# A list scheduler that counts eight transfers under way on SyncE's queue: one return trip in eight transfers instead of three, and pieces in another order

## The chip, the cores and the metric

The kernel runs on one core of one Trainium2 chip. The metric is the time of one execution on the device in microseconds (us). The kernel before took 271.07, 270.63 and 270.41 us in three runs, median 270.63. Another execution, not one of these three, was profiled: 271.06 us.

## The reference

The reference is a trunk of two layers over 256 tokens with D = 1024 features, all in fp32. Each layer normalises x, projects it to ten column groups with one matrix, runs three groups of attention heads side by side, gates them and projects back:

```python
for layer in range(DEPTH):
    h = rms_norm(x, norm_g[layer])
    proj = jnp.einsum('btd,dc->btc', h, w_in[layer])
    sb_q, sb_k, sb_v, sb_g, mb_q, mb_k, mb_v, mb_g, mem_q, mem_g = jnp.split(proj, split_at, axis=-1)
    o_sb = stick_breaking_attention(sb_q, sb_k, sb_v) * jax.nn.silu(sb_g)
    o_mb = moba_attention(rotary(mb_q), rotary(mb_k), mb_v) * jax.nn.silu(mb_g)
    m = rms_norm(mem, mem_norm_g[layer])
    mk, mv = jnp.split(jnp.einsum('bmd,dc->bmc', m, w_mem_kv[layer]), 2, axis=-1)
    o_mem = memory_attention(mem_q, mk, mv) * jax.nn.silu(mem_g)
    mixed = jnp.concatenate([o_sb, o_mb, o_mem], axis=-1)
    x = x + jnp.einsum('btc,cd->btd', mixed, w_out[layer])
return rms_norm(x, final_norm_g)
```

(The splitting into heads is left out.) There are six sb heads (stick breaking), six mb heads (here one causal softmax, since 256 tokens are one block) and four mem heads, which look at 256 memory tokens; a head has 64 features.

## The kernel before

**Products.** A product in fp32 is made of three matmuls in a narrower type. Every operand is split into a high part (a cast) and a low part (the operand less the cast), and hi x hi, hi x lo and lo x hi are summed in one PSUM bank. Where a piece is named in `DBL`, the high and low parts of the weights lie side by side, and one matmul of 512 columns and one of 256 do the work of three of 256.

**Weights.** They come from HBM in 114 chunks of 768 columns or so (128 partitions). A chunk is loaded into one of six raw buffers (`dma_chunk`, its DMA is issued at L366 on SyncE's queue), cast to its high part on ScalarE or VectorE (`hi_task`, L275), and the low part is subtracted on VectorE (`lo_task`, L281). Seven pairs of high and low parts are held (`hl`). The load of the next chunk into a raw buffer is issued when the subtraction that read that buffer is done, so a load on SyncE's queue often waits for VectorE.

**Attention.** Heads are worked on in pairs: sb 0 to 2, mb 0 to 2, mem 0 and 1. `pair_scores` makes the scores of a pair on TensorE in a smaller matmul shape (64 rows). Softmax or stick breaking then run on ScalarE and VectorE. The weights of the attention must be transposed for the second product. This is done in two steps. `pair_turn` transposes blocks of 32 x 32 on VectorE into a tile D (L843). Then `trip` writes D to a tile Z in memory outside the core's own (the *dump*, L996) and reads it back with the blocks in place (the *return*, L1007), into F or T; the profile prints F and T for the same kind of tile, by the name under which its memory was set up. The return is four transfers, one for each 32 partitions, or eight of half the size where the trip's name stands in `HALVES`. `pair_task` makes the second product (weights x values) in the shape 128 x 64, and then on VectorE multiplies it with the gate and splits it into mxhi and mxlo for the output projection (wo0, wo1, wo2).

**What sets the order.** The kernel is built by a list scheduler (`Sched`). Each task is a generator that says which engine, which buffers and which named values its next step needs. The scheduler holds a clock per engine and a cost model, and again and again picks the step that can start first; among steps that can start within a slack (`SLACK`, `SLACK_PE`) the lower priority number wins (`PRI`, `P_*`). The weights' chunks follow the list `ORDER` of each layer; `SCG` and `PVG` say which pairs' scores and second products are made together, `GATES` which gate columns are worked on together; `HOLD` and `SPARE2` bound how long and with how many banks a group is held back. The hardware then runs each engine's list in that order, and semaphores keep it correct. In the cost model a transfer occupies SyncE for 450 ns and then a shared bandwidth (`queue`), whatever number of transfers is under way.

**Around the change.** SyncE's queue holds 170 rows: weight loads, x and memory loads (`uT<-xT`, `uT<-memT`), dumps and returns. Near 80 to 120 us of the profile, the trips of the three mb pairs and the two mem pairs of layer 0 stand there between the loads of layer 1's memory tokens (memT, four transfers) and those of w_out.

Of the kernel before, what the change touches and what calls it, by code (L numbers as in the profile page):

```python
# [27 lines left out]
RAW = 6  # L28
KORD = ((4, 5, 0, 1, 2, 3, 6, 7), (6, 7, 4, 5, 0, 1, 2, 3))
LAT_SAME, LAT_CROSS = 130.0, 240.0  # L30
PE_LATE = 368.2
NORM_LATE = 542.1
DG_LATE = 1595.9
COLD = 3900.0
PRI = {"sb": (12, 16), "mb": (2, 14), "mem": (54, 40)}
P_EV = 37
P_H0 = -8
P_RX = 27
P_M0 = 62
P_RM = 2  # L40
P_M1 = 55
URG = 2
X_AT = {5: 4, 6: 5, 7: 6, 8: 7}
CST_AT = 12
X0_AT = 6
X1_AT = 13
DMA_GBS = 330.0
SP_ISSUE = 450.0
POOL_ISSUE = 1000.0
POOL_TRIP = 5500.0  # L50
DMA_LAT = 2200.0
DMA_GBS_1K = 285.0
TRIP_LAT = 1500.0
MEM_AT = 1
ORDER = (["sb_qk", "mb_k", "mb_q", "mem_q", "mv", "sb_g", "mk", "mb_v", "mb_g", "sb_v", "mem_g"],
         ["mv", "mk", "mb_q", "mb_k", "mem_q", "sb_q", "sb_k", "mb_g", "mb_v", "sb_v", "mem_g", "sb_g"])
GATES = {"sb_g": ((0,), (1,), (2,)), "mb_g": ((0, 1), (2,)), "mem_g": ((0,), (1,))}
SCG = (((("mem", 1), ("mb", 0), ("sb", 2)), (("sb", 0), ("sb", 1)), (("mb", 1),), (("mb", 2), ("mem", 0))),
       ((("sb", 1), ("mb", 2), ("sb", 2)), (("sb", 0), ("mb", 0), ("mb", 1)), (("mem", 0), ("mem", 1))))
PVG = (((("mem", 0), ("mem", 1)), (("mb", 0), ("mb", 2), ("mb", 1), ("sb", 2)), (("sb", 1), ("sb", 0))),  # L60
       ((("sb", 2),), (("mb", 2), ("sb", 0), ("sb", 1)), (("mb", 0), ("mb", 1), ("mem", 1), ("mem", 0))))
HOLD = 25950.0
HALVES = [("F", 0, "mem", 0), ("F", 0, "mb", 1), ("F", 0, "mb", 2)]
CROWD = 1
SPARE1 = 2
SPARE2 = 1
SUMP = (1, 2)
DBL = (("mem_g", 0), ("mb_g", 1), ("mb_g", 0), ("mem_q", 1), ("mk", 1), ("sb_qk", 0), ("sb_q", 1), ("mk", 0), ("sb_g", 1))
DVE_W = 231.1
AHEAD = 1  # L70
DVE_HI = 718.2
SLACK_PE = 7.9
SLACK = 64.5


def _free(ap):
    n = 1
    for d in ap.shape[1:]:
        n *= d
    return n  # L80
# [18 lines left out]
class Sched:  # L99
# [37 lines left out]
    def _avail(self, k, eng):  # L137
# [21 lines left out]
        if cond is not None and not cond():  # L159
            return None  # L160
        return t + r.get("late", PE_LATE) if eng == "pe" and k.gen.__name__ != "main" else t

# [59 lines left out]
def hybrid_trunk(ctx: ExitStack, tc: tile.TileContext, x, mem, norm_g, w_in, w_mem_kv, w_out,  # L222
# [5 lines left out]
    S = Sched()  # L228
# [131 lines left out]
    def queue(nbytes, run, now):  # L360

        dma_t["t"] = max(dma_t["t"], now) + nbytes / (380.0 if run >= 3072 else DMA_GBS if run > 1024 else DMA_GBS_1K)
        return dma_t["t"] + DMA_LAT

    def dma(dst, src, name=None, q=None, now=0.0):
        (q or nc.sync).dma_start(dst, src)  # L366
        if q is None:
            S.T["sp"] = max(S.T["sp"], now) + SP_ISSUE
        t = queue(_free(dst) * 4 * dst.shape[0], dst.shape[-1] * 4, now)
        if name:  # L370
            S.ready[name] = t

# [239 lines left out]
    def norm_task(l, t, H, done):  # L612
# [3 lines left out]
        for q in range(2):  # L616
            s = slice(q * 512, (q + 1) * 512)
            _, (w,) = yield R("dve", need=[("gb", 0)], alloc=["w"])
            stt(w, src[:, s], r, gb[:, s], OP.mult, OP.mult)
            _, (pt,) = yield R("pe", alloc=["bank"], late=NORM_LATE)  # L620
            for i in range(4):
# [370 lines left out]
    def trip(D, F, e, name, need=(), alloc=()):  # L992

        _, (Z,) = yield R("sp", alloc=["Z"])
        Zv = Z[:, :4 * e]
        nc.sync.dma_start(Zv, D[:, :4 * e])  # L996
        S.op("sp", SP_ISSUE)
        t = queue(2048 * e, 4096, S.cur.t) + TRIP_LAT
        S.res["D"].items.append((t, None, D))
        S.ready[("dump",) + name] = t  # L1000
        _, bufs = yield R("sp", need=[("dump",) + name] + list(need), alloc=alloc)
        F = bufs[0] if alloc else F
        Fv = F[:, :4 * e].rearrange("p (i e) -> p i e", i=4)
        for j in range(4):
            for i0 in range(0, 4, 2 if name in HALVES else 4):
                i1 = i0 + (2 if name in HALVES else 4)
                nc.sync.dma_start(Fv[32 * j:32 * j + 32, i0:i1],  # L1007
                                  Zv.rearrange("(i r) (j e) -> j r i e", i=4, j=4)[j, :, i0:i1])
                S.op("sp", SP_ISSUE)
        t = queue(2048 * e, 1024, S.cur.t) + TRIP_LAT  # L1010
        S.res["Z"].items.append((t, None, Z))
        S.ready[name] = t
        return F
# [90 lines left out]
    def main():  # L1104
# [26 lines left out]
        for l in range(DEPTH):  # L1131
# [34 lines left out]
            for h in range(SBH):  # L1166
                S.spawn(sb_head(l, h) if sums(l, "sb", h // 2) else scan_head(l, h), PRI["sb"][1] + h)
            for h in range(MEMH):
                S.spawn(soft_head(l, h, "mem"), PRI["mem"][1] + h)
            for h in range(SBH):  # L1170
                S.spawn(soft_head(l, h, "mb"), PRI["mb"][1] + h)
            for kind, n in (("sb", 3), ("mb", 3), ("mem", 2)):
                for c in range(n):
                    S.spawn(pair_scores(l, kind, c), PRI[kind][0] + 2)
                    S.spawn(pair_sums(l, c) if sums(l, kind, c) else pair_turn(l, kind, c), PRI[kind][0] + 1)
                    S.spawn(pair_task(l, kind, c), PRI[kind][0])
            if l == 0:
# [145 lines left out]
```

## Time and profile before

| | |
|---|---|
| time of the profiled execution | 271.06 us |
| its span, first to last instruction | 269.0 us |
| median of three other runs | 270.63 us (270.41 to 271.07) |
| TensorE matmuls (PE) | 261.0 us, 97% |
| TensorE weight loads (PEld) | 241.0 us, 90% |
| VectorE (DVE) | 229.4 us, 85% |
| ScalarE (ACT) | 197.9 us, 74% |
| GpSimd (POOL) | 7.3 us, 3% |
| granted TensorE clock | 0.995 of full speed |
| moved by DMA | 65.49 MB, mean 243 GB/s |

The difference of 271.06 and 269.0 lies around the span. In the rows of the profile a line starts with the start time and the length in us; `x8` is the number of instructions; `out<-in` are the tiles that an instruction writes and reads; a bracket at the end is the time its engine sat idle ahead of it and what ended that. SPq is SyncE's queue, which issues DMAs; a row of it tells how long the issue took, not the transfer.

### The profile page before, as it was taken

The page shows a single profiled execution, that of the slowest core. Times are in us where ns is not written, and L with a number is a line of the kernel's source. Part 1 is how long each engine was busy: PE and PEld are TensorE (multiplying, and loading weights), DVE is VectorE, ACT ScalarE, POOL GpSimd, SP SyncE. Part 2 cuts the span into 40 slices and gives each one's busy share as a digit, 9 for nine tenths or more (in the row PEclk, how much of TensorE's full clock was granted, in tenths as well). Part 3 has the DMA queues.
Part 4 walks back from the last instruction along what each step waited for, and adds up shares of the span by engine and source line. Part 5 has one row for each costly group of instructions (what it writes and reads, how often), then busy time and mean ns, then how long its engine had stood idle before and what let it go on. Part 6 is the DMA issues. An engine that isn't in the chain of part 4 may idle for free.

```text
span 269.0 us, 5193 instructions
## 1 busy us (share of the span) xinstructions
PE 261.0 (97%) x1733; PEld 241.0 (90%) x1733; DVE 229.4 (85%) x532; ACT 197.9 (74%) x462; POOL 7.3 (3%) x19
## 2 busy tenths in 40 slices
PE   8999999999999997999999999999999999999992
PEld 5889999999898995998999999889989989889991
DVE  4778889999999997995889678699999999996282
ACT  3798786799989897681887446476999995985053
POOL 0002100100000000000000000000000000000000
PEclk9999999999999999999999999999999999999998
DMA  7999989988858779894588755867899896964004
GB/s 219 363 403 395 387 279 286 322 255 287 239 190 251 244 197 333 267 251 159 133 272 283 234 182 219 274 207 247 268 265 267 271 305 178 279 232 139 0 0 156
DMA packets 50665, 65.49 MB, mean 243 GB/s; under 512 B 4240, under 2 KB 46608, under 8 KB 50640
## 3 DMA queue, kind: packets, MB, share of 16 engines
q1 hardware_dynamic: 49552, 63.08, 73.9%
q0 software_dynamic: 512, 1.31, 1.6%
q10 hardware_dynamic: 576, 0.79, 0.9%
q8 instruction: 13, 0.21, 0.3%
q14 instruction: 12, 0.10, 0.1%
HBM read 56.51 MB, written 8.65 MB: 242 GB/s over the span
## 4 chain that ended last, share of the span: by engine, by line
PE 94%; DMA 2%; ACT 1%; DVE 1%; SPq 1%; issue 0%; DVEq 0%
PE bank L258 93%; DMA T<-Z 2%; PE bank L264 1%; SPq L1007 1%; ACT ga L277 0%; ACT ss L277 0%; ACT junk L277 0%; DVE ga L285 0%; DVE xs L289 0%; DVE gT L281 0%; DVE st L809 0%; DVEq L1319 0%; SPq L366 0%; DVE junk L1107 0%; ACT sb_v L277 0%
## 5 line engine op out<-in xcount | busy, mean ns | idle before, releaser
L281 DVE TENSOR_TENSOR hl<-raw,hl 128x768 fp32r<-128x768 f32 (+3 forms) x114 | 101.4, 897 | 9.3 <-ACT hl L275 8.8
L258 PE MATMUL bank<-T,hl 128*128 128x256 f32 (+1 forms) x662 | 106.7, 320 | 0.0
L258 PEld LDWEIGHTS bank<-T,hl 128*128 128x128 f32 x662 | 94.1, 192 | 10.2 <-issue 1.8
L275 ACT CAST hl<-raw 128x768 fp32r<-128x768 f32 (+2 forms) x108 | 83.9, 795 | 11.2 <-PE bank L258 8.2
L258 PE MATMUL bank<-hl,T 128*128 128x384 f32 (+1 forms) x480 | 80.7, 325 | 0.0
L258 PEld LDWEIGHTS bank<-hl,T 128*128 128x128 f32 x480 | 78.5, 188 | 1.0 <-issue 0.4
L258 PE MATMUL bank<-hl,mxhi 128*128 128x384 f32 (+1 forms) x192 | 45.0, 318 | 0.0
L258 PEld LDWEIGHTS bank<-hl,mxhi 128*128 128x128 f32 x192 | 33.3, 189 | 0.6 <-issue 0.6
L258 PE MATMUL bank<-hl,mxlo 128*128 128x384 f32 (+1 forms) x96 | 30.4, 317 | 0.0
L277 ACT ACTIVATE w<-w,st 128x256 f32<-128x256 f32 (+1 forms) x44 | 18.9, 464 | 2.4 <-DVE st L796 2.2
L277 ACT ACTIVATE junk<-xs 128x384 bf16<-128x384 f32 (+2 forms) x15 | 8.0, 531 | 16.6 <-DVE xs L281 16.0
L277 ACT ACTIVATE ga<-ga 128x256 f32<-128x256 f32 (+1 forms) x42 | 18.5, 446 | 1.1 <-DVE ga L285 0.7
L258 PEld LDWEIGHTS bank<-hl,mxlo 128*128 128x128 f32 x96 | 18.1, 189 | 0.1
L843 DVE STREAM_TRANSPOSE D<-w 128x384 f32<-128x384 f32 (+1 forms) x28 | 17.0, 606 | 0.9 <-ACT w L277 0.9
L277 ACT ACTIVATE T<-uT,gc 128x256 fp32r<-128x256 f32 x24 | 11.5, 500 | 2.1 <-DMA uT<-xT_dram 2.1
L285 DVE SCALAR_TENSOR_TENSOR T<-uT,gc,T 128x256 fp32r<-128x256 f32 x24 | 11.5, 478 | 0.7 <-ACT T L277 0.7
L281 DVE TENSOR_TENSOR xs<-bank,xs 128x384 f32<-128x384 f32 (+1 forms) x11 | 5.7, 518 | 7.2 <-PE bank L258 7.1
L277 ACT ACTIVATE a<-a 128x384 f32<-128x384 f32 x24 | 11.8, 523 | 0.1
L281 DVE TENSOR_TENSOR ev<-bank,gT 128x256 f32<-128x256 f32 x16 | 6.6, 417 | 4.2 <-PE bank L258 4.1
L277 ACT ACTIVATE a<-bank 128x384 f32<-128x384 f32 x20 | 9.4, 485 | 0.1
L776 DVE TENSOR_TENSOR_SCAN a<-a,a 128x256 f32<-128x256 f32 (+1 forms) x16 | 8.5, 536 | 0.0
L796 DVE CUSTOM_DVE_ANT_0 w<-bank,cmask 128x128 f32<-128x128 f32 (+1 forms) x24 | 7.5, 348 | 0.2 <-PE bank L258 0.2
(120 smaller groups left out, 237.2 us busy)
## 6 DMA issues: line engine op xcount, KB each, us to landing
raw<-in_w_in_dram SPq DMA_DIRECT2D x70, 384.0 KB, 4.4
raw<-in_w_out_dram SPq DMA_DIRECT2D x18, 384.0 KB, 4.9
Z<-D SPq DMA_DIRECT2D x14, 384.0 KB, 4.2
raw<-in_w_mem_kv_dram SPq DMA_DIRECT2D x8, 384.0 KB, 4.7
uT<-memT_dram SPq DMA_DIRECT2D x8, 256.0 KB, 6.4
Z<-D SPq DMA_DIRECT2D x4, 512.0 KB, 6.3
F<-Z SPq DMA_DIRECT2D x16, 96.0 KB, 4.6
T<-Z SPq DMA_DIRECT2D x16, 96.0 KB, 4.1
```

Source lines behind the costliest of these rows:

```text
L258: nc.tensor.matmul(out, lhsT=lhsT, rhs=rhs, start=start, stop=stop, **kw)
L264: nc.tensor.transpose(out, in_, idt)
L275: nc.scalar.copy(out, in_)
L277: nc.scalar.activation(out, in_, func, **kw)
L281: nc.vector.tensor_tensor(out, a, b, op=op)
L285: nc.vector.scalar_tensor_tensor(out, a, s, b, op0=op0, op1=op1)
L776: nc.vector.tensor_tensor_scan(a[:, r0:r1], a[:, r0:r1], u[:, r0:r1], 0.0, OP.add, OP.add)
L796: nc.vector.tensor_tensor_reduce(w[:, r0:r1], sc[:, r0:r1], cmask[:, 256 - r1 + r0:256], -1.0, 3.0e38, OP.add, OP.min, st[:, t:t + 1])
L843: nc.vector.transpose(o, w[:, :n * 128].rearrange("p (m j r) -> p m j r", j=4, r=32))
L1007: nc.sync.dma_start(Fv[32 * j:32 * j + 32, i0:i1], Zv.rearrange("(i r) (j e) -> j r i e", i=4, j=4)[j, :, i0:i1])
```

## The change

The planner's model of SyncE gets a list of the landing times of all transfers that were issued on that queue. An issue is not put earlier than the landing of the transfer issued eight before it (`RING = 8`). A return's cost is counted for each of its four or eight transfers, where it was counted as one lump behind them. `HALVES`, the trips that come back in eight transfers, has one entry (the last mem pair of layer 0) where it had three. The numbers that steer the planner are others: priorities, slacks, the order of pieces and of groups. No operation of the arithmetic is another one.

```diff
+RING = 8
-HALVES = [("F", 0, "mem", 0), ("F", 0, "mb", 1), ("F", 0, "mb", 2)]
+HALVES = [("F", 0, "mem", 1)]
-MEM_AT = 1
-ORDER = (["sb_qk", "mb_k", "mb_q", "mem_q", "mv", "sb_g", "mk", "mb_v", "mb_g", "sb_v", "mem_g"],
-         ["mv", "mk", "mb_q", "mb_k", "mem_q", "sb_q", "sb_k", "mb_g", "mb_v", "sb_v", "mem_g", "sb_g"])
-GATES = {"sb_g": ((0,), (1,), (2,)), "mb_g": ((0, 1), (2,)), "mem_g": ((0,), (1,))}
+MEM_AT = 0
+ORDER = (["sb_qk", "mb_k", "mb_q", "mv", "mem_q", "sb_g", "mk", "sb_v", "mb_g", "mb_v", "mem_g"],
+         ["mv", "mk", "mb_q", "mb_k", "mem_q", "mem_g", "sb_q", "sb_k", "mb_g", "mb_v", "sb_v", "sb_g"])
+GATES = {"sb_g": ((0,), (1,), (2,)), "mb_g": ((0,), (1, 2)), "mem_g": ((0,), (1,))}
...
-DBL = (("mem_g", 0), ("mb_g", 1), ("mb_g", 0), ("mem_q", 1), ("mk", 1), ("sb_qk", 0), ("sb_q", 1), ("mk", 0), ("sb_g", 1))
+DBL = (("mem_g", 0), ("mb_g", 1), ("mb_g", 0), ("mk", 1), ("mk", 0), ("sb_qk", 0), ("mem_g", 1), ("mem_q", 1), ("sb_q", 1))
...
     def dma(dst, src, name=None, q=None, now=0.0):
         (q or nc.sync).dma_start(dst, src)
         if q is None:
-            S.T["sp"] = max(S.T["sp"], now) + SP_ISSUE
+            S.T["sp"] = max(S.T["sp"], now, ring[-RING]) + SP_ISSUE
+            now = max(now, S.T["sp"] - SP_ISSUE)
         t = queue(_free(dst) * 4 * dst.shape[0], dst.shape[-1] * 4, now)
+        if q is None:
+            ring.append(t)
...
         nc.sync.dma_start(Zv, D[:, :4 * e])
-        S.op("sp", SP_ISSUE)
-        t = queue(2048 * e, 4096, S.cur.t) + TRIP_LAT
+        S.op("sp", SP_ISSUE + max(0.0, ring[-RING] - max(S.T["sp"], S.cur.t0)))
+        t = queue(2048 * e, 4096, S.cur.t)
+        ring.append(t)
+        t += TRIP_LAT
...
-                S.op("sp", SP_ISSUE)
-        t = queue(2048 * e, 1024, S.cur.t) + TRIP_LAT
+                S.op("sp", SP_ISSUE + max(0.0, ring[-RING] - max(S.T["sp"], S.cur.t0)))
+                t = queue(2048 * e * (i1 - i0) // 16, 1024, S.cur.t)
+                ring.append(t)
+        t += TRIP_LAT
```

Left out are the numbers of the cost model and priorities, `SCG`, `PVG`, `HOLD` and `SPARE2`; what they do shows in the order. Both kernels put 170 rows on SyncE's queue.

First place, SyncE's queue before, from the loads of memT to the trips of the mb pairs of layer 0. Z0, Z1 and Z2 are the dumps of mb pairs 0, 1 and 2, T1 is the tile they return to (one name for several parts of memory), and the sizes at the end are partitions x blocks x elements.

```order
L366 DMA uT_72<-memT_dram 128x2x256 x4
L366 DMA raw4_92<-in_w_out_dram 128x2x384
L1007 DMA T1_74<-Z0_124 32x2x192 x8
L996 DMA Z2_126<-D1_121 128x768
L1007 DMA T1_74<-Z1_125 32x2x192 x8
L366 DMA raw5_93<-in_w_out_dram 128x2x384
L366 DMA raw0_88<-in_w_out_dram 128x2x384
L366 DMA raw1_89<-in_w_out_dram 128x2x384
L366 DMA raw2_90<-in_w_out_dram 128x2x384
L1007 DMA T1_74<-Z2_126 32x4x192 x4
L996 DMA Z0_124<-D0_120 128x1024
```

The same place of SyncE's queue now; the Z0 of 1024 columns is the dump of mem pair 0.

```order
L1015 DMA T1_74<-Z0_124 32x4x192 x4
L369 DMA raw4_92<-in_w_out_dram 128x2x384
L1015 DMA T1_74<-Z1_125 32x4x192 x4
L369 DMA uT_72<-memT_dram 128x2x256 x4
L369 DMA raw5_93<-in_w_out_dram 128x2x384
L1002 DMA Z2_126<-D0_120 128x768
L1002 DMA Z0_124<-D1_121 128x1024
L369 DMA raw0_88<-in_w_out_dram 128x2x384
L369 DMA raw1_89<-in_w_out_dram 128x2x384
L369 DMA raw2_90<-in_w_out_dram 128x2x384
L1015 DMA T1_74<-Z2_126 32x4x192 x4
L1015 DMA T1_74<-Z0_124 32x4x256 x4
```

The returns of pairs 0 and 1 have moved ahead of memT and are four transfers each; the dump of pair 2 has moved behind memT, and the dump and return of mem pair 0 have moved up beside those of mb pair 2.

Second place, SyncE's queue a few rows on, before: the trips of the two mem pairs, Z0 for pair 0 and Z1 for pair 1.

```order
L996 DMA Z1_125<-D1_121 128x1024
L366 DMA raw5_93<-in_w_out_dram 128x2x384
L366 DMA raw0_88<-in_w_out_dram 128x2x256
L1007 DMA T1_74<-Z0_124 32x2x256 x8
L366 DMA raw1_89<-in_w_out_dram 128x3x256
L1007 DMA T1_74<-Z1_125 32x4x256 x4
```

And now:

```order
L369 DMA raw3_91<-in_w_out_dram 128x2x384
L369 DMA raw4_92<-in_w_out_dram 128x2x384
L1002 DMA Z1_125<-D0_120 128x1024
L369 DMA raw5_93<-in_w_out_dram 128x2x384
L369 DMA raw0_88<-in_w_out_dram 128x2x256
L1015 DMA T1_74<-Z1_125 32x2x256 x8
```

The trip of mem pair 1 comes back in eight transfers behind the load of raw0, and pair 0's return no longer stands ahead of it there.

Third place, TensorE's list before, where the second products of the mb pairs of layer 0 stand. T1 with mb_v is a pair of mb, F with sb_v a pair of sb; hl with T0 is a weight chunk in the full shape.

```order
L258 MATMUL bank3_104<-T0_73,hl1_95 128x512
L258 MATMUL bank3_104<-T0_73,hl1_95 128x256
L258 MATMUL bank2_103<-T1_74,mb_v_82 64x256 x2
L258 MATMUL bank2_103<-T1_74,mb_v_82 64x128 x2
L258 MATMUL bank7_108<-T1_74,mb_v_82 64x256 x2
L258 MATMUL bank7_108<-T1_74,mb_v_82 64x128 x2
L258 MATMUL bank4_105<-T1_74,mb_v_82 64x256 x2
L258 MATMUL bank4_105<-T1_74,mb_v_82 64x128 x2
L258 MATMUL bank1_102<-F0_118,sb_v_81 64x256 x2
L258 MATMUL bank1_102<-F0_118,sb_v_81 64x128 x2
```

Now TensorE takes two mb pairs and one sb pair first, where it took two sb pairs (in the middle of the chunks hl1 to hl3 that go to one bank), and eighteen full-shape matmuls later this second group:

```order
L259 MATMUL bank3_104<-T0_73,hl2_96 128x512
L259 MATMUL bank3_104<-T0_73,hl2_96 128x256
L259 MATMUL bank7_108<-T1_74,mb_v_82 64x256 x2
L259 MATMUL bank7_108<-T1_74,mb_v_82 64x128 x2
L259 MATMUL bank5_106<-F1_119,sb_v_81 64x256 x2
L259 MATMUL bank5_106<-F1_119,sb_v_81 64x128 x2
L259 MATMUL bank6_107<-F0_118,sb_v_81 64x256 x2
L259 MATMUL bank6_107<-F0_118,sb_v_81 64x128 x2
L259 MATMUL bank0_101<-T1_74,mv_83 64x256 x4
```

One mb pair, two sb pairs and mem pair 0 stand in it; mem pair 1 follows alone some forty rows later, where both mem pairs stood together.

More of the change, by code (lines that the diff above doesn't have):

```diff
@@ L30 @@
 LAT_SAME, LAT_CROSS = 130.0, 240.0
-PE_LATE = 368.2
-NORM_LATE = 542.1
-DG_LATE = 1595.9
+PE_LATE = 375.1
+NORM_LATE = 1029.7
+DG_LATE = 885.3
 COLD = 3900.0
-PRI = {"sb": (12, 16), "mb": (2, 14), "mem": (54, 40)}
+PRI = {"sb": (6, 16), "mb": (-6, 14), "mem": (36, 44)}
 P_EV = 37
 P_H0 = -8
[L38 to L41, printed above, removed]
+P_RX = 32
+P_M0 = 40
+P_RM = 7
+P_M1 = 10
 URG = 2
 X_AT = {5: 4, 6: 5, 7: 6, 8: 7}
-CST_AT = 12
-X0_AT = 6
-X1_AT = 13
+CST_AT = 13
+X0_AT = 7
+X1_AT = 12
 DMA_GBS = 330.0
+RING = 8
 SP_ISSUE = 450.0
@@ L53 @@
 TRIP_LAT = 1500.0
-MEM_AT = 1
-ORDER = (["sb_qk", "mb_k", "mb_q", "mem_q", "mv", "sb_g", "mk", "mb_v", "mb_g", "sb_v", "mem_g"],
-         ["mv", "mk", "mb_q", "mb_k", "mem_q", "sb_q", "sb_k", "mb_g", "mb_v", "sb_v", "mem_g", "sb_g"])
-GATES = {"sb_g": ((0,), (1,), (2,)), "mb_g": ((0, 1), (2,)), "mem_g": ((0,), (1,))}
-SCG = (((("mem", 1), ("mb", 0), ("sb", 2)), (("sb", 0), ("sb", 1)), (("mb", 1),), (("mb", 2), ("mem", 0))),
+MEM_AT = 0
+ORDER = (["sb_qk", "mb_k", "mb_q", "mv", "mem_q", "sb_g", "mk", "sb_v", "mb_g", "mb_v", "mem_g"],
+         ["mv", "mk", "mb_q", "mb_k", "mem_q", "mem_g", "sb_q", "sb_k", "mb_g", "mb_v", "sb_v", "sb_g"])
+GATES = {"sb_g": ((0,), (1,), (2,)), "mb_g": ((0,), (1, 2)), "mem_g": ((0,), (1,))}
+SCG = (((("mem", 1), ("mb", 0), ("sb", 2)), (("sb", 0), ("sb", 1)), (("mb", 1), ("mem", 0)), (("mb", 2),)),
        ((("sb", 1), ("mb", 2), ("sb", 2)), (("sb", 0), ("mb", 0), ("mb", 1)), (("mem", 0), ("mem", 1))))
-PVG = (((("mem", 0), ("mem", 1)), (("mb", 0), ("mb", 2), ("mb", 1), ("sb", 2)), (("sb", 1), ("sb", 0))),
+PVG = (((("mem", 1),), (("mb", 2), ("sb", 1)), (("mem", 0), ("sb", 0), ("sb", 2), ("mb", 0)), (("mb", 1),)),
        ((("sb", 2),), (("mb", 2), ("sb", 0), ("sb", 1)), (("mb", 0), ("mb", 1), ("mem", 1), ("mem", 0))))
-HOLD = 25950.0
-HALVES = [("F", 0, "mem", 0), ("F", 0, "mb", 1), ("F", 0, "mb", 2)]
+HOLD = 18370.6
+HALVES = [("F", 0, "mem", 1)]
 CROWD = 1
 SPARE1 = 2
-SPARE2 = 1
+SPARE2 = 2
 SUMP = (1, 2)
-DBL = (("mem_g", 0), ("mb_g", 1), ("mb_g", 0), ("mem_q", 1), ("mk", 1), ("sb_qk", 0), ("sb_q", 1), ("mk", 0), ("sb_g", 1))
[L69 to L73, printed above, removed]
+DBL = (("mem_g", 0), ("mb_g", 1), ("mb_g", 0), ("mk", 1), ("mk", 0), ("sb_qk", 0), ("mem_g", 1), ("mem_q", 1), ("sb_q", 1))
+DVE_W = 204.1
+AHEAD = 3
+DVE_HI = 739.2
+SLACK_PE = 12.2
+SLACK = 75.4
 def _free(ap):
@@ L363, in queue @@
         return dma_t["t"] + DMA_LAT
+    ring = [0.0] * RING
     def dma(dst, src, name=None, q=None, now=0.0):
```

## The prediction

> **What bounds the kernel now.** I read the page first: the engines' busy time and the 40 slices.
>
> ```profile
> span 269.0 us, 5193 instructions
> PE 261.0 (97%) x1733; PEld 241.0 (90%) x1733; DVE 229.4 (85%) x532; ACT 197.9 (74%) x462; POOL 7.3 (3%) x19
> PE   8999999999999997999999999999999999999992
> ```
>
> TensorE is busy for 261.0 of 269.0 us and is below 9 tenths in three slices only: the head, the sixteenth (101 to 108 us) and the tail. The head and the tail hold the same operations after the change as before. So all that a new order can win is in the sixteenth slice, apart from the number of the matmuls. The table of stretches of time says how much that is, and the waits of PE say for what.
>
> ```profile
> 50.00:90.00 40.00, 40.00 (x281) 36.85 (x280) 39.22 (x108) 37.84 (x98) 1.49 (x3) 1.00 0.83 259
> 90.00:100.00 10.00, 10.00 (x60) 9.96 (x59) 9.94 (x21) 8.72 (x22) 0.00 (x0) 1.00 0.66 170
> 100.00:110.00 10.00, 8.53 (x71) 6.61 (x71) 8.58 (x22) 6.13 (x14) 0.00 (x0) 1.00 1.02 355
> PE bank L258 <- DMA T<-Z: 1.5, 1, 1.5
> PE bank L258 <- DVE junk L1107: 1.2, 1, 1.2
> ```
>
> The columns are the stretch, its length, then busy time of PE, weight load, VectorE, ScalarE and GpSimd, granted clock, DMA share and GB/s. PE lost 10.00 - 8.53 = 1.47 us between 100 and 110 us, and the second list has only one other wait, at the very start. The clock is 1.00 there. Next, the timeline of PE around the hole (start, length, instructions, idle time ahead).
>
> ```profile
> 92.14 7.51 PE L258 MATMUL bank<-hl,T 128*128 128x384 f32 x42
> 99.49 1.55 PE L258 MATMUL bank<-T,hl 128*128 128x512 f32 x8
> 100.97 1.52 PE L258 MATMUL bank<-F,sb_v 128*64 128x256 f32 x16
> 102.42 2.03 PE L258 MATMUL bank<-T,hl 128*128 128x512 f32 x10
> 105.92 2.17 PE L258 MATMUL bank<-T,mb_v 128*64 128x256 f32 x24 [1.47 <-DMA T<-Z]
> 107.89 0.85 PE L258 MATMUL bank<-F,sb_v 128*64 128x256 f32 x8
> ```
>
> TensorE wanted to begin the products of the three mb pairs with mb_v at 102.42 + 2.03 = 104.45 and began at 105.92. Last, the chain of waits through it, and SyncE's queue (issues only).
>
> ```profile
> 98.38 0.47 SPq L1007
> ...
> 99.87 5.91 DMA T<-Z
> ...
> 105.92 32.53 PE bank L258 x227
> ```
>
> ```profile
> 82.66 1.96 SPq L366 DMA_DIRECT2D uT<-memT_dram  x4
> 84.72 0.40 SPq L366 DMA_DIRECT2D raw<-in_w_out_dram  x1
> 85.17 6.53 SPq L1007 DMA_DIRECT2D T<-Z  x8
> 91.80 0.68 SPq L996 DMA_DIRECT2D Z<-D  x1
> 92.52 3.78 SPq L1007 DMA_DIRECT2D T<-Z  x8
> 96.40 1.93 SPq L366 DMA_DIRECT2D raw<-in_w_out_dram  x4
> 98.38 1.92 SPq L1007 DMA_DIRECT2D T<-Z  x4
> ```
>
> ```profile
> 86.86 0.57 DVE L843 STREAM_TRANSPOSE D<-w 128x384 f32<-128x384 f32 x1
> SPq L1007 <- DMA uT<-memT_dram: 2.3, 4, 0.7
> SPq L996 <- DMA raw<-in_w_out_dram: 1.3, 1, 1.3
> ```
>
> The issues of three narrow stretches (count, KB each, median us from issue to landing: the third pair's dump, the second pair's return, the third pair's return) close the picture.
>
> ```profile
> Z<-D SPq DMA_DIRECT2D x1, 384.0 KB, 2.7
> T<-Z SPq DMA_DIRECT2D x8, 48.0 KB, 2.0
> T<-Z SPq DMA_DIRECT2D x4, 96.0 KB, 6.1
> ```
>
> The late thing is the third mb pair (mb, 2). VectorE had its transposed weights in D at 86.86 + 0.57 = 87.43. Its dump went out only at 91.80, 4.4 us later, because the first pair's return in eight transfers stood ahead and took 6.53 us to issue instead of the 3.78 us that the second pair's eight took. The waits of SyncE's queue say why: four of those issues, and the dump itself, waited for the landing of transfers issued earlier (memT and a w_out load) that have nothing to do with them. No more than eight were under way. The dump took 2.7 us more. Then the third pair's return stood behind the second's eight transfers and four loads; its last piece, issued at 99.87, landed 5.91 us later, at 105.78. So the bound is TensorE, and the one hole is made by a queue.
>
> **The change, part by part.** (1) *The count of eight in the planner.* It adds no instruction; it only makes the planner see what the rows above show. Its effect is the order.
>
> (2) *The order at the hole.* The first two mb returns go back to four transfers and stand ahead of memT; the third pair's dump follows memT and one load; its return comes behind three loads. By the rows: the first return can go at 82.66, where memT began. Then 4 + 1 + 4 + 4 + 1 = 14 issues stand ahead of the dump, against 13 before. At 0.47 us each (98.38 row) they are 6.6 us, which gives 89.3; with the limit I put the dump at 89.5 to 91.8 and its landing, 2.7 us on, at 92.2 to 94.5. The dump of the first mem pair and three loads follow, some 2 us. The return goes at 94 to 96 and lands, at the 6.1 us of the last row (the far end; 2.0 us with an empty queue), by 100 to 102.
>
> What TensorE asks of it moves too. At 100.97 it now takes mb pairs 0 and 1 and one sb pair; these returns go out near 83 and 86 and land, at the same 6.1 us, by 92 to 93. The third mb pair is asked for later: that first group of 24 products takes the 107.89 - 105.92 = 1.97 us of the old one, and 18 full-shape matmuls follow at (100.97 - 99.49)/8 = 185 ns, so 100.97 + 1.97 + 3.33 = 106.3. Margin: 106.3 - 102 = 4.3 us at the bad end. So the wait goes: 1.47 us of idle, and some 0.07 us more, since a group that waits for nothing starts a little ahead of the modelled end of the one before (100.97 against 99.49 + 1.55 = 101.04). I take -1.5 us; bounds -1.6 and 0.
>
> (3) *What is late next.* Two things get nearer. First mb_v's own evacuation: mb_v is now the piece that ends at 99.49, where sb_v ended before, and VectorE scales it by the token factors before 100.97. That leaves 1.48 us for an operation of about 0.57 us (as the 86.86 row, 384 columns too) on an engine that is busy 9.94 of 10.00 us there. Counting the queue of VectorE in the new order, I put its end at 100.2, 0.8 us in time. I take 0, bounds 0 and +1.5 us. Second the last mem pair's return, now in eight transfers:
>
> ```profile
> 100.29 0.93 DVE L281 TENSOR_TENSOR hl<-raw,hl 128x768 fp32r<-128x768 f32 x1
> 104.72 0.96 DVE L281 TENSOR_TENSOR hl<-raw,hl 128x768 fp32r<-128x768 f32 x1
> 106.81 6.20 SPq L1007 DMA_DIRECT2D T<-Z  x8
> T<-Z SPq DMA_DIRECT2D x8, 64.0 KB, 5.4
> 120.73 1.95 PE L258 MATMUL bank<-T,mv 128*64 128x256 f32 x16
> ```
>
> Its dump stands behind two loads that wait for VectorE's subtractions near 100.3 and 102 (issue at 102.5, landing by 107). Its return stands behind one more load, which waits for the subtraction that ended at 104.72 + 0.96 = 105.7 before and has four more operations of the attention ahead of it now, each 0.5 us or so: 107.6. Eight issues took 3.78 us at best and 6.20 us with the limit: last issue 110.9 to 113.3. Landing: 112.9 at the 2.0 us of an empty queue, 118.7 at 5.4. I take 115, nearer to the first, since fewer loads are queued ahead of it. TensorE asks for it one group earlier than before, 120.73 - 1.5 - 1.5 = 117.7. One wait gone is the first 1.5; the other is that this pair's group now stands about 1.5 us earlier in PE's list. Margin 2.7 us, so I take 0, bounds 0 and +1.0.
>
> (4) *Split returns.* The Trainium skill, Perfetto Trace Analysis, section DMA Optimizations, says that splitting transfers may let parts start sooner when the DMA engines are mostly idle, which speaks against undoing two of the three splits. The rows agree where the queue was free (2.0 us for 48 KB) and not where eight stood in it (6.53 us to issue them); by that rule the two mb returns would land about 2 us later than in eight pieces, inside the 8 us they have, and the sum stays.
>
> Another rule denies the gain. The Trainium skill, SBUF — State Buffer, section The DMA setup-cost knee, fits a transfer at about 2 us plus its bytes over 436 GB/s. By it the 96 KB return issued at 99.87 lands at an estimated 102.1, ahead of 104.45, there is no wait to remove, and the time stays at 270.6. The trace has 5.91 us and a wait of 1.47, so I go by the trace.
>
> (5) *Matmuls.* In the list of pieces whose matmuls are merged, sb_g of layer 1 (three column groups) gives way to mem_g of layer 1 (two): eight k-steps more are done as three matmuls of 256 columns, not as 512 + 256.
>
> ```profile
> 39.48 5.91 PE L258 MATMUL bank<-T,hl 128*128 128x256 f32 x48
> 45.23 3.04 PE L258 MATMUL bank<-hl,T 128*128 128x256 f32 x24
> ```
>
> Forty-eight narrow ones take 45.23 - 39.48 = 5.75 us, 120 ns each, 360 for three. The eight mixed ones from 99.49 to 100.97 take 185 ns each, 370 a pair, a change of shape included. Eight times the difference is -0.08, and without the change of shape (0.1 us once at most) up to +0.1; I take 0.05. TensorE leaves the full shape for the attention as often as before (12 times), so that is 0.
>
> (6) *The rest*: gate groups of mb 1 + 2 instead of 2 + 1, sb_v ahead of mb_g, mv ahead of mem_q, mem_g of layer 1 earlier, later x loads. Each is covered by the weights' lead: no matmul waited for a weight in the list above. The cover costs what VectorE lacks; between 50 and 90 us it is idle 40.00 - 39.22 = 0.78 us. VectorE's list gets ten instructions shorter, which at the mean of 229.4/532 = 0.43 us would be 4 us; mostly small ones go, and I count 2. A gain is excluded, since PE waits there for nothing; I take 0, bounds 0 and +1.5 (the cover gone and 0.8 us to spare). In layer 1 the returns are asked for in another order; no row shows a wait there now, and I take 0.
>
> Sum: -1.5 + 0.05, so -1.45, rounded to -1.5. The profiled execution took 271.06 us (span 269.0 and 2.06 around it), 0.43 above the median of 270.63. By the sum it comes to 269.6, and the median to 270.63 - 1.5 = 269.1. Less than 0.3% (0.8 us) couldn't be told from no change.
>
> **The rivals.** A: *the wait moves.* VectorE, full from 50 to 100 us, comes late with mb_v or with a weight chunk of the mb gates that now follow the scores. For it: the 39.22 of 40.00 and a margin of 0.8 us. Against it: VectorE has about 2 us less to do. A lag of 2 us there gives back 1.2, of 2.5 us all: 269.8 to 270.7.
>
> B: *slower, by the last mem return.* It turns the other way if the eight pieces land after 117.7 + 1.5 = 119.2, because from there the new wait exceeds the old one. Their issue begins behind a load that hangs on VectorE, and if each waits for a landing as the three slowest of the 106.81 row did (2.9 us for w_out landings in three issues, the row below), that is 2.9/3 + 0.45 = 1.4 us each: 107.6 + 8 x 1.4 + 2.0 = 120.8. TensorE then waits 3.1 us: 270.63 - 1.5 + 3.1 = 272.2. For it:
>
> ```profile
> SPq L1007 <- DMA raw<-in_w_out_dram: 2.9, 3, 1.2
> ```
>
> Against it: only three issues in eight were held so.
>
> C: *the change doesn't do what it says.* The third mb return still lands after 106.3, since it has as many issues ahead as before; 4.3 us must have gone wrong. Then the wait stays in part: 270 to 270.6. That returns land fast anyway, so that nothing could be won, gets no chance beside the 5.91 us row.
>
> **How the numbers follow.** My forecast 0.70: the margins are 0.8 us at mb_v and 2.7 us or more at the returns. A 0.17, B 0.09, C 0.04. The likeliest case gives 269.1, and alone 268.7 to 269.6 (the gain between 1.9 and 1.0: 0.1 to 0.3 of unknown in the matmuls and changes of shape, 0.3 from run to run). To reach 8 in 10 the range takes in two thirds of A: 268.6 to 270.5. Faster by over 0.8 us means under 269.8: the forecast and a little of A, 0.70. Within it: most of A, and C, 0.20. Slower: B and a little from places that I have no row for, 0.10.
>
> **What would show it.** Right: the list of PE's waits has no row for T<-Z, the stretch 100 to 110 us shows PE busy 10.00, SyncE's queue shows the third dump before 91.8 and its return landing by 102, the last mem return lands by about 115, and the chain holds no DMA but at the ends. Step 3 is wrong if PE waits at mb_v or at mv; step 6 if it waits for hl between 70 and 100 us. The prediction is wrong if PE's idle time between 90 and 125 us sums to over 0.7 us, or if the sum of its busy time grows by more than 0.3.

## The result and the profile after

The changed kernel takes 269.05 us (median of 7 runs, 268.18 to 269.57), the kernel before 270.98 us in its 7 runs beside it. One of these seven took 274.98 us, far from the others, and is left out of the ratio as a slow run. The ratio is 0.9933 with a 95% interval of 0.9916 to 0.9951, so it is faster by 0.5 to 0.8%. The profiled execution took 269.23 us with a span of 267.3 us, 1.7 us less than before. By code the trip that the prediction calls the third, (mb, 2), is that of mb pair 0, and the two ahead of it are those of pairs 1 and 2; the buffers Z0 to Z2 had given the names. The text below calls it the third trip.

The page of the changed kernel, busy times and the row of PE in 40 slices:

```profile
span 267.3 us, 5185 instructions
...
PE 260.8 (98%) x1741; PEld 241.1 (90%) x1741; DVE 227.4 (85%) x526; ACT 199.4 (75%) x466; POOL 7.2 (3%) x19
...
PE   8999999999999999999999999999999999999992
```

The stretch of the hole (columns as before), and then the whole list of PE's waits:

```profile
100.00:110.00 10.00, 10.00 (x84) 7.44 (x84) 10.00 (x26) 7.29 (x15) 0.00 (x0) 1.00 0.86 243
```

```profile
PE bank L259 <- DVE junk L1117: 1.2, 1, 1.2
```

The sixteenth slice is full, the stretch that had 8.53 us of PE has 10.00, and the wait for T<-Z is gone from the list; only the one at the very start is left. The timeline of PE at the place:

```profile
99.26 1.55 PE L259 MATMUL bank<-T,hl 128*128 128x512 f32 x8
100.74 1.52 PE L259 MATMUL bank<-T,mb_v 128*64 128x256 f32 x16
...
106.19 0.87 PE L259 MATMUL bank<-T,mb_v 128*64 128x256 f32 x8
106.89 1.47 PE L259 MATMUL bank<-F,sb_v 128*64 128x256 f32 x16
108.19 1.03 PE L259 MATMUL bank<-T,mv 128*64 128x256 f32 x8
...
117.22 1.08 PE L259 MATMUL bank<-T,mv 128*64 128x256 f32 x8
```

No row has a bracket. The third mb pair is used at 106.19, the mem pairs at 108.19 and 117.22. SyncE's queue there, and three of its stretches by issue and landing (count, KB each, median us to landing): the third dump, the third return, the last mem return.

```profile
82.04 1.83 SPq L1015 DMA_DIRECT2D T<-Z  x4
83.98 0.39 SPq L369 DMA_DIRECT2D raw<-in_w_out_dram  x1
84.47 2.34 SPq L1015 DMA_DIRECT2D T<-Z  x4
86.91 2.98 SPq L369 DMA_DIRECT2D uT<-memT_dram  x4
90.04 0.37 SPq L369 DMA_DIRECT2D raw<-in_w_out_dram  x1
90.45 0.94 SPq L1002 DMA_DIRECT2D Z<-D  x2
92.52 2.77 SPq L369 DMA_DIRECT2D raw<-in_w_out_dram  x3
96.89 7.10 SPq L1015 DMA_DIRECT2D T<-Z  x8
...
110.56 4.47 SPq L1015 DMA_DIRECT2D T<-Z  x8
```

```profile
Z<-D SPq DMA_DIRECT2D x1, 384.0 KB, 6.4
...
T<-Z SPq DMA_DIRECT2D x4, 96.0 KB, 6.7
...
T<-Z SPq DMA_DIRECT2D x8, 64.0 KB, 2.0
```

The third dump goes at 90.45, 1.35 us sooner than before. Its return's last piece is issued at 98.22 and lands at 104.5, against 105.8 before. So the return itself came 1.3 us sooner, nearly the 1.47 us that TensorE had lost, and TensorE's new order, which asks at 106.19 and not at 104.45, leaves 1.7 us to spare. By these rows either would have done nearly all of it alone: the old landing (105.8) is ahead of the new need (106.19), and the new landing (104.5) would have left some 0.2 us of wait at the old one. What each is worth alone the trace can't tell; the experiments can.

### The profile page after: what moved, and what is told of

Its sections match the earlier page's. It is cut to its first block, busy times and chain, and to the rows that moved or that the text cites. A ratio compares the mean times of both kernels' runs of the same rounds, so it can differ in the third digit from the quotient of the medians.

```text
span 267.3 us, 5185 instructions
## 1 busy us (share of the span) xinstructions
PE 260.8 (98%) x1741; PEld 241.1 (90%) x1741; DVE 227.4 (85%) x526; ACT 199.4 (75%) x466; POOL 7.2 (3%) x19
## 4 chain that ended last, share of the span: by engine, by line
PE 98%; ACT 0%; DVE 0%; DVEq 0%; issue 0%
PE bank L259 97%; PE bank L265 1%; ACT ss L278 0%; ACT junk L278 0%; DVE xs L290 0%; DVEq L1329 0%; DVE junk L1117 0%
## 5 line engine op out<-in xcount | busy, mean ns | idle before, releaser
L276 ACT CAST hl<-raw 128x768 fp32r<-128x768 f32 (+3 forms) x109 | 85.5, 799 | 9.1 <-PE bank L259 4.9
L282 DVE TENSOR_TENSOR gT<-gT,ga 128x256 f32<-128x256 f32 (+1 forms) x14 | 6.4, 455 | 1.6 <-ACT ga L278 1.4
```

Of the source, the lines that this page charges most:

```text
L276: nc.scalar.copy(out, in_)
L282: nc.vector.tensor_tensor(out, a, b, op=op)
```

## The experiments

Three theories stood against each other. *Queue*: the third trip was late because other issues stood ahead of it on SyncE's queue, each taking its 0.4 us and some waiting for a landing. *Bandwidth*: it was late because of the bytes under way. *Order*: the gain came from TensorE asking later. All ratios below are to the kernel before, with 95% intervals.

**1. One edit to the kernel before: one trip split.**

```diff
-HALVES = [("F", 0, "mem", 0), ("F", 0, "mb", 1), ("F", 0, "mb", 2)]
+HALVES = [("F", 0, "mem", 1)]
```

> The kernel before with one edit: only the last mem pair returns in eight transfers, the two mb pairs and the first mem pair in four. TensorE's list is the same up to the mb products. Queue theory (the third mb trip is late because issues stand ahead of it on SyncE's queue): its dump goes at about 91.5 us as before, since eight issues stand ahead of it again, but its return no longer stands behind a second set of eight; it is issued at 95.5 to 97 and lands at 101.5 to 103, before TensorE asks at 104.4. The wait of 1.5 us goes, time 269.1 to 269.6. Bandwidth theory (the DMA engines are full, the return lands late wherever it stands): landing near 105, wait at least 1.0, time within 0.3% of the kernel before. Order theory (the gain came from TensorE asking for the pair later): nothing moves on TensorE, so the wait stays and the time too.

Measured: 269.18 us, ratio 0.9928 (0.9912 to 0.9945): the whole gain, with the old order on TensorE and no count of eight. PE's row at the mb products, then SyncE's queue:

```profile
104.08 2.17 PE L258 MATMUL bank<-T,mb_v 128*64 128x256 f32 x24
```

```profile
84.86 6.11 SPq L1007 DMA_DIRECT2D T<-Z  x8
91.20 0.34 SPq L996 DMA_DIRECT2D Z<-D  x1
91.64 3.45 SPq L366 DMA_DIRECT2D raw<-in_w_out_dram  x4
95.19 2.00 SPq L1007 DMA_DIRECT2D T<-Z  x4
```

The dump goes about when it did (91.20, before 91.80), but the return no longer stands behind a second eight: issued from 95.19, not 98.38, landed by 102.7. TensorE's three mb pairs start at 104.08 with no wait. TensorE's list is the old one up to the mem pairs, which it takes three matmuls sooner. No new order on TensorE at the hole is needed for the gain.

**2. The third trip on another queue.** All other lists of the kernel before are word for word kept.

```diff
+        q = nc.gpsimd if name == ("F", 0, "mb", 0) else nc.sync
-        nc.sync.dma_start(Zv, D[:, :4 * e])
+        q.dma_start(Zv, D[:, :4 * e])
...
-                nc.sync.dma_start(Fv[32 * j:32 * j + 32, i0:i1],
+                q.dma_start(Fv[32 * j:32 * j + 32, i0:i1],
```

> The kernel before with one edit: the dump and the return of the third mb pair of layer 0 are issued on GpSimd's queue, which is idle there. All other lists are word for word the same. Queue theory: the dump goes soon after VectorE is done at 87.4, the return lands by 99, the wait of 1.5 us at the mb products goes, and the time is 269.1 to 269.6; at most 0.5 us comes back at the mem products, whose return landed at 119.7 and will be asked for at 119.2. Bandwidth theory: the return shares the DMA engines with the same bytes and lands within a microsecond of 105; wait at least 0.5 us, time 270 or more. Order theory: TensorE's list is the same, the wait stays, 270.6 to 271.

Measured: 268.93 us, ratio 0.9923 (0.9905 to 0.9941). GpSimd's queue, with the idle time ahead in the bracket:

```profile
87.83 0.56 POOL L997 DMA_DIRECT2D Z<-D  x1 [31.04 <-DMA uT<-memT_dram]
92.80 2.21 POOL L1008 DMA_DIRECT2D T<-Z  x4 [4.40 <-DMA Z<-D]
```

The dump goes at 87.83, 0.3 us after VectorE is done (87.54 in this run), while SyncE is busy with sixteen issues from 85.28 to 95.50; the return is issued by 95.0 and lands by 97.5. The wait was made by the place in SyncE's queue.

**3. TensorE asks later.** SyncE's list is word for word the old one; behind the hole VectorE's and ScalarE's lists change their order too.

```diff
                           form="col", crowd=1 if len(group) > 1 or kind == "mem" and c == 1 else CROWD, need=need,
+                          late=PE_LATE + (1500.0 if (l, kind) == (0, "mb") else 0.0))
```

> The kernel before with one edit: the planner is told to put the products of the three mb pairs of layer 0 later (1.5 us on its own clock), so TensorE asks for the third pair some 2.5 us later and for the mem pairs some 0.6 us earlier. SyncE's list is word for word the same. Order theory: the wait goes and the time is 269.1. Queue theory: the returns land when they did (105.8 and 119.7); the mb wait shrinks to 0 to 0.1 us, but TensorE asks for the mem pairs at 118.6 and waits there 0.5 to 1.1 us; time 269.6 to 270.2. Bandwidth theory: as the queue theory.

Measured: 270.11 us, ratio 0.9966 (0.9951 to 0.9982), half of the gain.

```profile
104.47 0.87 PE L258 MATMUL bank<-F,sb_v 128*64 128x256 f32 x8
...
106.23 2.17 PE L258 MATMUL bank<-T,mb_v 128*64 128x256 f32 x24
...
110.20 0.34 PE L258 MATMUL bank<-hl,mxhi 128*128 128x384 f32 x1
...
119.19 2.01 PE L258 MATMUL bank<-T,mv 128*64 128x256 f32 x16
```

The wait at the mb products goes in this way too, though the return landed when it did (106.1): the order can take the wait away as well, but it earns less. What it cost is in the rows. The sb pair that stood with the mb pairs now is a group by itself, so TensorE leaves the full shape once more (13 times, not 12), and the matmuls from here to the first with mxhi take 110.20 - 104.47 = 5.73 us. The same matmuls took 111.25 - 105.92 = 5.33 us in the kernel before, by its row:

```profile
111.25 0.34 PE L258 MATMUL bank<-hl,mxhi 128*128 128x384 f32 x1
```

So 0.4 of the 1.47 us is given back, and the span fell by 1.0 us (268.1 against 269.0). The expected wait at the mem pairs is not in the list of waits: TensorE asked at 119.2, not at 118.6, and the last return, which landed at 119.9, can have been needed by the second half of the sixteen matmuls only.

**4. The count of eight alone**, with the old numbers and the old three splits.

```diff
+RING = 8
...
-            S.T["sp"] = max(S.T["sp"], now) + SP_ISSUE
+            S.T["sp"] = max(S.T["sp"], now, ring[-RING]) + SP_ISSUE
```

> The kernel before with the planner's count of eight transfers and nothing else: the same numbers, the same three trips in eight transfers. The plan then puts the mb products ten full-shape matmuls later on TensorE (asked for at about 106.0, the third pair 1.4 us after that) and the third return right behind the second. If the count is what matters: no wait on TensorE, 269.1 to 269.4, as the whole change. If the numbers and the splits matter: a wait of 0.5 us or more stays at a return, 269.8 or more.

Measured: 271.15 us, ratio 1.0011 (0.9985 to 1.0037): nothing gained. Two rows of PE:

```profile
106.05 2.17 PE L259 MATMUL bank<-T,mb_v 128*64 128x256 f32 x24
...
110.69 0.45 PE L259 MATMUL bank<-hl,mxhi 128*128 128x384 f32 x1 [0.92 <-DVE mxhi L297]
```

The mb wait is gone and another stands ahead of 110.69: with the products at 106.05, VectorE has gated and split them only when TensorE already wants them for the output projection. TensorE's busy time grew as well, from 261.0 to 262.2 us; over the whole run TensorE's weight loads waited 2.0 us for mxhi and 1.1 us for mxlo, which the list of the kernel before has nowhere. The count makes the planner's picture of SyncE truer, and the plan drawn from it is not better.

**5. The suspected cost doubled**: the first two returns of the kernel before in sixteen transfers each, the same bytes, all other rows kept.

```diff
+                step = 1 if name in (("F", 0, "mb", 1), ("F", 0, "mb", 2)) else i1 - i0
+                for i2 in range(i0, i1, step):
```

> The kernel before with one edit: the returns of mb pairs 1 and 2 go out in sixteen transfers each, not eight, of the same bytes; every other row of every list is the same. The third pair's trip so has sixteen more issues ahead of it. Queue theory (issues count): its dump moves from 91.8 to about 95 and its return's last issue from 99.9 to 105 to 107; it lands at 108 to 111 and TensorE waits 3.5 to 6.5 us instead of 1.5: 272.6 to 276. Bandwidth theory (bytes count): the same landing within 1 us, the same time within 0.3%. Skill's rule that smaller pieces finish sooner: the first two returns land sooner, the third is not later, time the same or less.

Measured: 280.3 us, ratio 1.0344 (1.0313 to 1.0375). PE's row at the mb products, three rows of SyncE's queue, and the two stretches after the wait, each from its own view:

```profile
113.27 4.11 PE L258 MATMUL bank<-T,mb_v 128*64 128x256 f32 x24 [8.68 <-DMA T<-Z]
```

```profile
85.33 10.54 SPq L1009 DMA_DIRECT2D T<-Z  x16
95.96 0.37 SPq L996 DMA_DIRECT2D Z<-D  x1
96.37 7.44 SPq L1009 DMA_DIRECT2D T<-Z  x16
```

```profile
113.30:118.30 5.00, 5.00 (x32) 3.54 (x32) 2.25 (x7) 0.00 (x0) 0.00 (x0) 0.53 1.05 399
118.30:122.00 3.70, 3.70 (x23) 3.39 (x22) 3.58 (x10) 2.61 (x5) 0.00 (x0) 1.00 0.67 143
```

The issues moved as expected (dump 95.96, return from 105.9); the landing, at 113.1, came 2 to 5 us later than I had put it: behind four loads the last piece took 5.8 us, as in the kernel before (5.91), where I had allowed less. It is the number of issues that counts, with the bytes unchanged. The wait grew from 1.47 to 8.68 us, and for 5 us after it the granted clock was 0.53: (8.68 - 1.47) + 5 x 0.47 = 9.6 us, near the 9.4 us measured. The rule on splitting that the prediction took from the Trainium skill, Perfetto Trace Analysis, section DMA Optimizations, asks that the DMA engines be mostly idle, and here they are not (busy share 0.83 from 50 to 90 us of the kernel before, 0.66 from 90 to 100). Splitting gains nothing here: a piece of the second return took some 1.7 us where it had taken 2.0, but the two returns as a whole landed at 97.1 and 105.1, where in eight pieces they had landed at 93.3 and 97.7, and the trip behind them came late with them.

**6. The changed kernel with the old splits**, its plan untouched: mb 1, mb 2 and mem 0 in eight transfers, mem 1 in four.

```diff
+EMIT = [("F", 0, "mem", 0), ("F", 0, "mb", 1), ("F", 0, "mb", 2)]
...
+                step = 2 if name in EMIT else 4
```

> The changed kernel with its plan untouched, but the trips of mb 1, mb 2 and mem 0 are issued in eight transfers and that of mem 1 in four, as the old list had it; all other rows are the same. Queue theory: twelve more issues stand ahead of the return of the third mb pair's and the first mem pair's last pieces. The dump moves from 90.5 to 92 to 93.5, the return lands at 105 to 107 against the need at 106.2, the mem pair's at 107.5 to 109 against 108.2: a wait of 0 to 1.5 us, 269.0 to 270.5. Order theory (TensorE's new order alone carries the gain, with all the margin it needs): 269.05 within 0.3%, no wait.

Measured: a ratio of 1.0130 (1.0088 to 1.0173), with runs from 272.6 to 278.1 us; the profile is of the longest of these, so its figures are those of that execution alone. PE's waits, and the row of VectorE behind the second:

```profile
PE bank L260 <- DMA T<-Z: 3.0, 2, 2.5
PE bank L260 <- DVE mb_v L291: 1.9, 1, 1.9
```

```profile
101.03 0.71 DVE L850 STREAM_TRANSPOSE D<-w 128x512 f32<-128x512 f32 x1 [3.95 <-DMA Z<-D]
```

The dump moved to 93.8, as expected, but I had missed who else waits for it: the tile D is free only when the dump has landed, VectorE's next transpose stood still for 3.95 us for it, and the evacuation of mb_v behind that came 1.9 us late. The 3.0 us of the first row are at the mem pairs; during the longer of its two waits the granted clock went down to half (last section). So the new order gains only with the splits taken out, which the order theory did not allow for.

**7. The changed kernel with no split**, `EMIT = []`, the same plan.

> The changed kernel with its plan untouched, the last mem pair's return issued in four transfers of 128 KB, not eight of 64. It landed at 116.67 in eight, 0.55 us before TensorE asked at 117.2. Queue theory: the queue is free there (2 to 5 under way), so four are issued in 1.9 us instead of 4.5 and land by 115.5 to 116.7: no wait, 269.05 within 0.3%. Skill's rule that smaller pieces finish sooner: four land later, at 117 to 118.5, a wait of up to 1.3 us, up to 270.3.

Measured: 269.62 us, ratio 0.9958 (0.9939 to 0.9977). No wait of PE but the first. The return by its landing:

```profile
T<-Z SPq DMA_DIRECT2D x4, 128.0 KB, 3.3
```

Four pieces were issued from 108.68 (the last at 110.7) and were there by 114.0, 2.8 us before TensorE asked at 116.8; the eight had landed 0.55 us before. Most of this is not the edit: SyncE's list up to this return is that of the changed kernel, and yet the dump landed at 108.6, where it had landed at 110.49, so the return could start 1.9 us sooner. From the first issue to the last landing it is 5.3 us in four pieces and 6.1 in eight. The one split that the change keeps isn't needed. The interval overlaps that of the change, so the 0.2% between the two can't be told from nothing; in this profile TensorE was done sooner (261.5 against 262.0 us), and the time from its last matmul to the end was longer (6.6 against 5.3 us).

**8. The changed numbers without the count of eight.**

```diff
-PRI = {"sb": (12, 16), "mb": (2, 14), "mem": (54, 40)}
+PRI = {"sb": (6, 16), "mb": (-6, 14), "mem": (36, 44)}
...
-HALVES = [("F", 0, "mem", 0), ("F", 0, "mb", 1), ("F", 0, "mb", 2)]
+HALVES = [("F", 0, "mem", 1)]
```

> The kernel before with all the changed numbers (priorities, orders, groups, the one split) and without the count of eight. The plan puts the first mem pair's dump and return ahead of the third mb pair's. If the count is what makes the plan right: the third mb return lands at 106 or later against the need at 106.2, a wait of 0.3 to 1 us there, 269.4 to 270. If the numbers alone carry it: no wait, 269.05 within 0.3%.

Measured: 270.21 us, ratio 0.9977 (0.9960 to 0.9993). The waits of PE beside the first:

```profile
PE bank L259 <- DVE mxlo L282: 0.7, 1, 0.7
PE bank L259 <- DVE hl L297: 0.2, 1, 0.2
```

The third trip is in time, but in layer 1 (at 241.6 us) TensorE waits 0.7 us for VectorE. The third return landed at 105.7, 0.1 us before it was asked for, so the wait that I expected there is missing. The numbers fit the planner with the count better than the one without.

**9. memT on GpSimd's queue**, in the kernel before.

```diff
-            dma(uT[:, q * 2:q * 2 + 2, :], memT_r[:, q * 2:q * 2 + 2, :], ("memT", l, 2 * q), now=S.cur.t)
+            dma(uT[:, q * 2:q * 2 + 2, :], memT_r[:, q * 2:q * 2 + 2, :], ("memT", l, 2 * q), nc.gpsimd if l else None, now=S.cur.t)
```

> The kernel before with one edit: the four loads of layer 1's memory tokens (memT, 1 MB) are issued on GpSimd's queue. TensorE's, VectorE's and ScalarE's lists are word for word the same; on SyncE's queue both returns of eight now stand ahead of the third pair's dump (17 issues, where 13 stood). If eight are counted for each queue: the first return's issues no longer wait for memT, 16 returns and a load go out in 8 us from 82.5, the dump at 90.5 to 91.5, the third return is issued near 95 to 96.5 and lands by 103; no wait on TensorE, 269.1 to 269.6. If eight are counted over all queues, or bytes are what counts: the issues wait for memT as before, the dump goes at 94 or later, the return lands at 107 or later, a wait of 2.5 us or more, 271.5 or more.

Measured: 270.45 us, ratio 0.9989 (0.9965 to 1.0012); PE waits 0.82 us at the mb products and 0.4 us for a weight chunk. SyncE's queue, its waits between 82 and 95 us, and the landing of the first return:

```profile
82.86 4.17 SPq L1007 DMA_DIRECT2D T<-Z  x8
...
94.39 0.37 SPq L996 DMA_DIRECT2D Z<-D  x1
```

```profile
SPq L1007 <- DMA T<-Z: 2.1, 4, 0.8
```

```profile
T<-Z SPq DMA_DIRECT2D x8, 48.0 KB, 5.4
```

It came out between the two expectations. The first eight issues took 4.17 us, not 6.53, so memT's transfers on the other queue are not counted with SyncE's. But the pieces, with 1 MB of memT under way on the other queue, landed only after 5.4 us, and the second eight waited for the landing of the first. So the count is each queue's, and how fast it turns over hangs on how soon transfers land. The bandwidth theory has a share in the delay, not the whole.

**10. The kernel before with no split**, `HALVES = []`.

> The kernel before with no trip in eight transfers. Queue theory: as with one split left, the third return lands by 103 and the wait goes; the mem pairs are asked for nine matmuls sooner than with one split (near 117), and eight transfers of 128 KB issued from 105.9 land by 113: no wait, 269.0 to 269.4. Skill's rule that smaller pieces finish sooner: the returns land later than in eight, and a wait of 0.5 us or more is left somewhere, 269.7 or more.

Measured: 269.11 us, ratio 0.9936 (0.9912 to 0.9961), no wait but the first; PE's row:

```profile
104.07 2.17 PE L258 MATMUL bank<-T,mb_v 128*64 128x256 f32 x24
```

The return went at 95.2 again, as in the first experiment. The mb wait is gone with no split at all. The two plain edits (1 and 10), the other queue (2) and the whole change lie within each other's intervals (0.9923 to 0.9936). None beats the change by what can be told, and TensorE has no wait left in any of them.

## Why the prediction was right, point by point

The forecast was 269.1 us, the measured median is 269.05, and the mechanism is the one it gave: the wait of 1.47 us went, and nothing came in its place. That the medians agree to 0.05 us is luck in part: the base of 270.63 came from three runs, the six runs beside the change that the ratio uses have a median of 270.8, and the gain is nearer to 1.8 us than to the 1.5 of the sum. Its steps fared differently.

*The reading of the hole.* The prediction has the third dump itself wait for a w_out load, by the row of 1.3 us. That row belongs to the mem dump at 103.76; the third dump followed the issue ahead of it within 0.1 us. The issue that a w_out load held was the last of the first return's eight, in the stretch from 85 to 92.4 us of the kernel before:

```profile
SPq L1007 <- DMA raw<-in_w_out_dram: 0.8, 1, 0.8
```

The dump was late all the same because those eight were, so the sum stands. In rival B, too, the 2.9 us are not all of the return at 106.81: 0.8 of them are this row, and the return itself was held 2.1 us by w_out loads and 1.6 us by dumps, in four issues.

*The sum.* The span fell by 1.74 us: 1.5 from the wait, and about 0.2 that I had not counted. TensorE reached the place 0.23 us sooner already (the eight matmuls ahead of the products start at 99.26, not 99.49), spread over the first 100 us; no one row holds it. Executions differ by as much: with the old list up to there, TensorE got to this place 0.30 us sooner in experiment 1 and 0.11 us later in experiment 2. Shown by experiments 1, 2 and 10: the wait's 1.5 us is what the queue cost.

*The third trip.* The dump was forecast at 89.5 to 91.8 and went at 90.45. Its landing was mis-sized: 2.7 us was the row of a dump with only pieces of 48 KB under way ahead of it, and with 1 MB of memT under way it took 6.4. So the return landed at 104.5, not by 102. That this did no harm is due to the need at 106.19 (forecast 106.3): the margin was 1.7 us, not 4.3. Experiment 9 shows what I had left out, the bytes of the transfers ahead.

*mb_v.* Forecast to be ready at 100.2, 0.8 us ahead of its use. It was evacuated from 99.46 to 100.08 and used at 100.74:

```profile
99.46 0.62 DVE L290 TENSOR_SCALAR mb_v<-bank,rcx 128x384 f32<-128x384 f32 x1 [0.57 <-PE bank L259]
```

VectorE even waited for TensorE there. Rival A had this as its place; experiment 6 shows that it does decide once VectorE is held up ahead of it.

*The last mem return.* Forecast to land at 115 with 2.7 us to spare; it landed at 116.67, 0.55 us before its use at 117.22. Rival B turned slower from 119.2; the return was nearer to it than I had put it. The cause that I gave, landings in the way of the issues, was not the one: its issues began at 110.56, not 107.6, behind the load and behind its own dump, which landed at 110.49. With four transfers (experiment 7) the return has more room, though most of that was the execution's. One profile shows a margin of one execution: 0.55 us is less than the 1.9 us by which the same dump moved between two of them.

*Splits.* I priced the return to four transfers at 2 us of later landing inside an 8 us margin, and the effect of the split itself only through the order. Experiments 1, 5, 6 and 10 show that it is the lever: taking the splits out of the old kernel is worth the whole change, and putting them back into the new one makes it slower than the old. The rule from the Trainium skill, SBUF — State Buffer, section The DMA setup-cost knee, by which there was nothing to win, doesn't hold for transfers with others under way: returns of 96 KB took 6.7 us in the changed kernel where 2.2 was the estimate by it, and shortening the queue ahead won 0.7%.

*Matmuls.* Eight more, forecast +0.05 us; the lists have 1741 against 1733. TensorE's busy time is 260.8 us against 261.0, so this can't be told apart in the time.

*The rest.* By the pages VectorE has six instructions fewer (526 against 532), not ten; its busy time fell by the 2 us that I had counted.

*Point (1), the count.* I said that its effect is the order. Experiments 4 and 8 add that the count alone gives nothing, and the numbers alone about a third of the gain (0.2%).

## What to carry to other kernels

Read a late transfer back to its issue, and ask what stood ahead of it on that queue and how many: here one transfer's delay was a line of split transfers that nobody was waiting for, and taking out the split was worth as much as a new plan of the whole kernel. No split paid for itself in these runs, and with something urgent behind it on the queue it cost; in experiment 6 it delayed the dump that freed VectorE's tile as well. A better cost model is no gain by itself: check its plan for the next wait, on each engine. Where an issue waits for a transfer that it has nothing to do with, look which semaphore the two share (next section).

## What the runs showed of the hardware

SyncE's queue began no issue while eight earlier ones were under way: the most was seven, in all twelve traces, and in each 13 to 21 issues began within 0.04 us of the landing of the transfer eight before. The traces also show what held them, and it stands in the program. Each transfer raises a semaphore when it lands; SyncE's transfers take turns with eight of them (numbers 101, 102 and 104 to 109), and each of these issues, 200 in all, waits in its own instruction for the very semaphore that it will raise. GpSimd's transfers raise eight others (111 to 118), so its queue was not counted with SyncE's (experiments 2 and 9): in experiment 9 an issue on SyncE's queue began at 85.93 with eleven transfers under way, seven of SyncE's and four of GpSimd's. So the eight is a count of semaphores; what a queue would hold with more of them no run here shows, and more of them is a remedy that was not tried. In the changed kernel two of the eight issues of the row at 96.89 waited so for w_out loads:

```profile
SPq L1015 <- DMA raw<-in_w_out_dram: 3.6, 2, 2.0
```

A wait of 1.47 us on TensorE left the clock at 1.00 (stretch 100 to 110 us of the kernel before). The wait of 8.68 us was followed by 5 us at 0.53, and then 1.00 again. The Trainium skill, TensorE: Matmul & The Clock Gate, Part 1, says that the clock halves after an idle window of about 3.4 us and comes back after one of work; these two waits agree with it, the way back taking up to 5 us here. A third, in the profile of experiment 6, does not by its length:

```profile
122.78 1.98 PE L260 MATMUL bank<-T,mv 128*64 128x256 f32 x8 [2.51 <-DMA T<-Z]
...
124.60:129.00 4.40, 4.40 (x15) 4.32 (x14) 2.35 (x5) 0.27 (x1) 0.00 (x0) 0.50 0.95 321
```

After 2.51 us of idle time the clock was at half until 129 us, some 6 us. So a wait on this kernel can cost its own length, as the 1.47 us did, or 2 to 3 us more: 2.35 after the 8.68 us, some 6.2 x 0.50 = 3.1 after the 2.51. Where between the lengths the step lies, or what else it hangs on, these runs don't show.
